# Windowed attention on one core: query norm factors moved from the queries to the scores, and ALiBi distances formed by GpSimd two steps ahead

## The chip, the cores and the metric

One core of a Trainium2 chip runs the whole program. The metric is the device time of one execution in microseconds (us), as the median of several executions of the same compiled program. Five engines work beside each other: TensorE (PE, matmuls; PEld are its weight loads), VectorE (DVE), ScalarE (ACT), GpSimd (POOL) and SyncE (SP, which here issues transfers). Each takes its own instructions strictly in the order in which they were written for it, and waits on semaphores for what the others produce.

## The reference

Two layers on a 1024 x 1024 activation in float32. Layer 0 mixes tokens with a short gated convolution, layer 1 with sliding-window attention; each is followed by a SwiGLU block. What the change touches is the attention of layer 1:

```python
q = rmsnorm(q, q_gain)      # per head of 64
k = rmsnorm(k, k_gain)
scores = jnp.einsum('bnqkgd,bnskd->bnkgqs', qb, kw) * scale
dist = qi + BLOCK - kj      # 0 <= dist < 128 is kept
scores = scores - slopes * dist          # per query head
logits = concat([where(mask, scores, -inf), sink])
p = softmax(logits)[..., :-1]
out = einsum(p, v) @ w_o
```

Sixteen query heads of 64 share four key and value heads. The RMS norm of a query is one factor per head and token. It multiplies every score of that query, so that it can be applied before the product with the keys or after it.

## The kernel before

**Arithmetic.** Each float32 product is made of matmuls on two rounded pieces per operand, a high one and the remainder: a "split" is a cast to the high piece and a subtraction that gives the low one. Large projections use a scheme of seven products for eight.

**The stage.** The attention lies between about 985 and 1262 us of the span. First the keys, the values and the first query tiles are projected (`first_pairs`, until about 1027 us). Then come 64 units (i, b): i is a query tile of two heads (0 to 7), b a block of 128 queries (0 to 7). They run one per step, and since each unit's work is spread over four steps, several are under way at once. PE's time between the pieces of a unit is filled with granules of the query projection of later tiles, which is why the steps until about 1185 us carry matmuls of `three` (L1997) and the later ones carry the output projection.

**What sets the order.** The string `ORDER` (L60) is one step. Each letter calls a function on a unit, and what it issues goes into the queues of the engines in that order. For step n: S is `scores` of unit n (PE, L2234 and L2235, into one PSUM bank, P0), T is `turn` of unit n-2 (four PE transposes, L2277), M is `maxima` of unit n (DVE, L2249: score plus distance, times minus the slope, and the minimum with the sink, in one custom operation), E is `exponents` of unit n-1 (ACT, L2269), D is `divide_steps` of finished groups, H and L are `turn_hi` (ACT) and `turn_lo` (DVE, L2290) of unit n-2, V and O are `values` and `keep_o` of unit n-3, P is a piece of the projection, and k and K issue what `plan` has put on an agenda for the step or half a step before it. Since P0 is one bank, the scores of unit n+1 wait until the maxima of unit n have read it.

**The queries.** `keep_q` makes tile i ready for the scores, on the agenda after its projection is complete: squares (ACT), sums over each head (`head_stats`, L1678, PE with 2 columns), mean (`head_mean`, L1685), logarithm and exponential for a first guess (ACT), one Newton step (`head_guess` L1704 and L1706, `head_newton` L1710 and L1711, DVE with 16 columns). The factor is one number per token and head, with the tokens in the partitions, while the queries have their tokens in the columns. So the factor is spread over 512 columns by a GpSimd copy (`spread`, L1803), transposed four times by PE (`turn_blocks`, L1808) and multiplied onto the raw queries by DVE (`scale_rows`, L1813), each twice per tile. Only then are the queries split, in four parts: `part_hi` (ACT, L2165) and `part_lo` (GpSimd, L2170). The division by the sums of exponents uses the same `spread` and `turn_blocks`.

**GpSimd's other work.** It subtracts for the splits of the projection's weights (`split_granule`, L1941; the cast ahead of it, L1940, is on DVE or ACT), for the keys (L1878) and for the output projection, and makes two short steps of the softmax sums (L2332 and L2334).

**Buffers of the scores.** `score_buffers` (L1815) gives three buffers of 128 x 512; unit n uses buffer n mod 3, each of its two rows of 256 columns holding 192 live ones. The distances are one constant table of 192 columns that `maxima` reads for every unit.

## Time and profile before

| | |
|---|---|
| median of 3 runs | 1926.03 us (1925.07 to 1926.16) |
| span of the profiled execution | 1921.5 us |
| 960 to 1027 us: PE / DVE / POOL busy | 66.92 / 40.77 / 12.94 us of 67.00 |
| 1027 to 1230 us, the 64 units: PE / DVE / POOL busy | 197.41 / 168.67 / 114.72 us of 203.00 |
| 1230 to 1262 us: PE / DVE / POOL busy | 32.00 / 25.39 / 5.80 us of 32.00 |

The span counts from the first instruction to the last and is 4.5 us below the median. Busy time is the time in which at least one instruction of an engine ran. A high share says that an engine has little room, and not yet that it sets the end; that is read from the chain of waits and from what PE waits for. In a row of a group, the numbers behind the bar are the busy time in us, the mean duration of one in ns, and the idle time of that engine just before, with what ended it.

### The profile page before, as it was taken

The page shows a single profiled execution, that of the slowest core. Times are in us where ns is not written, and L with a number is a line of the kernel's source. Part 1 is how long each engine was busy: PE and PEld are TensorE (multiplying, and loading weights), DVE is VectorE, ACT ScalarE, POOL GpSimd, SP SyncE. Part 2 cuts the span into 40 slices and gives each one's busy share as a digit, 9 for nine tenths or more (in the row PEclk, how much of TensorE's full clock was granted, in tenths as well). Part 3 has the DMA queues.
Part 4 walks back from the last instruction along what each step waited for, and adds up shares of the span by engine and source line. Part 5 has one row for each costly group of instructions (what it writes and reads, how often), then busy time and mean ns, then how long its engine had stood idle before and what let it go on. Part 6 is the DMA issues. An engine that isn't in the chain of part 4 may idle for free.

```text
span 1921.5 us, 25423 instructions
## 1 busy us (share of the span) xinstructions
PE 1910.4 (99%) x9045; PEld 1595.6 (83%) x9045; DVE 1323.1 (69%) x2293; ACT 891.6 (46%) x1753; POOL 305.9 (16%) x391
## 2 busy tenths in 40 slices
PE   9999999999999999999999999999999999999999
PEld 7888888888888888888887888888888888888887
DVE  8998877975655666555767888788756665665543
ACT  5543464633333334444557787556333333344441
POOL 0011231011111100000015556310111111100000
PEclk9999999999999999999999999999999999999999
DMA  8896695387888647986374661232675575477562
GB/s 317 258 251 149 133 249 160 110 274 209 228 250 234 152 141 281 325 249 211 102 257 158 210 214 50 94 137 89 216 204 144 196 200 158 130 251 269 198 228 100
DMA packets 154910, 374.13 MB, mean 195 GB/s; under 512 B 15392, under 2 KB 26784, under 8 KB 154784
## 3 DMA queue, kind: packets, MB, share of 16 engines
q1 hardware_dynamic: 119392, 263.16, 40.1%
q0 software_dynamic: 35248, 109.33, 23.4%
q8 instruction: 71, 1.16, 0.2%
q14 instruction: 55, 0.45, 0.1%
q10 hardware_dynamic: 144, 0.03, 0.0%
HBM read 300.89 MB, written 149.42 MB: 234 GB/s over the span
## 4 chain that ended last, share of the span: by engine, by line
PE 96%; DVE 2%; ACT 1%; issue 1%; POOL 0%; DMA 0%; SPq 0%; POOLq 0%; ACTq 0%; DVEq 0%
PE acc L1004 16%; PE acc L1007 16%; PE acc L1005 16%; PE P L1004 10%; PE P L1005 10%; PE P L1007 10%; PE acc L172 3%; PE acc L1997 2%; PE P L1997 2%; PE acc L176 1%; PE P L2277 1%; PE P L1678 1%; PE P L1808 1%; PE acc L1137 1%; PE acc L1139 1%; PE acc L1138 1%
## 5 line engine op out<-in xcount | busy, mean ns | idle before, releaser
L1004 PE MATMUL acc<-XS,G 128*128 128x512 f32 x926 | 360.4, 389 | 0.0
L1005 PE MATMUL acc<-XS,G 128*128 128x512 f32 x926 | 360.2, 389 | 0.0
L1007 PE MATMUL acc<-XS,G 128*128 128x512 f32 x926 | 360.2, 389 | 0.0
L1004 PE MATMUL P<-A,G 128*128 128x512 f32 x550 | 214.1, 389 | 0.0
L1007 PE MATMUL P<-A,G 128*128 128x512 f32 x550 | 214.0, 389 | 0.0
L1005 PE MATMUL P<-A,G 128*128 128x512 f32 x550 | 214.0, 389 | 0.0
L1007 PEld LDWEIGHTS acc<-XS,G 128*128 128x128 f32 x926 | 173.8, 188 | 36.2
L1005 PEld LDWEIGHTS acc<-XS,G 128*128 128x128 f32 x926 | 173.8, 188 | 36.1
L1004 PEld LDWEIGHTS acc<-XS,G 128*128 128x128 f32 x926 | 173.8, 188 | 36.0
L1004 PE MATMUL acc<-A,G 128*128 128x512 f32 x442 | 172.1, 389 | 0.0
L1007 PE MATMUL acc<-A,G 128*128 128x512 f32 x442 | 172.0, 389 | 0.0
L1005 PE MATMUL acc<-A,G 128*128 128x512 f32 x442 | 171.9, 389 | 0.0
L938 DVE TENSOR_TENSOR G<-WL,G 128x512 fp32r<-128x512 f32 x168 | 115.2, 685 | 73.2 <-ACT G L937 73.2
L938 DVE TENSOR_TENSOR G<-WR,G 128x512 fp32r<-128x512 f32 (+1 forms) x216 | 144.4, 668 | 30.6 <-ACT G L937 30.6
L937 ACT CAST G<-WR 128x512 fp32r<-128x512 f32 (+1 forms) x216 | 130.5, 605 | 62.3 <-PE acc L1007 31.4
L937 ACT CAST G<-WH 128x512 fp32r<-128x512 f32 (+1 forms) x174 | 104.6, 601 | 88.5 <-PE acc L1007 38.2
L938 DVE TENSOR_TENSOR G<-WH,G 128x512 fp32r<-128x512 f32 (+1 forms) x174 | 115.6, 665 | 23.3 <-ACT G L937 23.2
L1339 ACT ACTIVATE G<-G 128x512 f32<-128x512 f32 x88 | 55.8, 634 | 158.5 <-DVE G L1436 152.7
L1007 PEld LDWEIGHTS P<-A,G 128*128 128x128 f32 x550 | 103.2, 188 | 21.5
L1004 PEld LDWEIGHTS P<-A,G 128*128 128x128 f32 x550 | 103.2, 188 | 21.4
L1005 PEld LDWEIGHTS P<-A,G 128*128 128x128 f32 x550 | 103.2, 188 | 21.4
L901 POOL DMA_DIRECT2D s<-s x68 | 60.0, 892 | 365.3 <-DMA s<-s 179.5
(414 smaller groups left out, 3794.2 us busy)
## 6 DMA issues: line engine op xcount, KB each, us to landing
G<-h SPq DMA_DIRECT2D x70, 512.0 KB, 4.5
s<-in_w_dn SPq DMA_DIRECT2D x32, 704.0 KB, 8.4
h<-X POOLq DMA_DIRECT2D x44, 512.0 KB, 4.8
s<-s POOLq DMA_DIRECT2D x32, 704.0 KB, 7.1
WR<-s SPq DMA_DIRECT2D x79, 256.0 KB, 3.9
WR<-in_w_gu SPq DMA_DIRECT2D x36, 512.0 KB, 5.1
WH<-in_w_gu SPq DMA_DIRECT2D x36, 512.0 KB, 4.2
XS<-q_ops SPq DMA_DIRECT2D x36, 512.0 KB, 5.1
```

Of the source, the lines that this page charges most:

```text
L172: pe.matmul(ps.half(h), wh, xs[:, j, c], start=first and j == 0, stop=False)
L176: pe.matmul(ps.half(h), wl, xs[:, 0, c], start=False, stop=last)
L901: nc.gpsimd.dma_start(dst[to], dst[of], accum_op=ALU.add)
L937: lambda: act.copy(out_hi, raw),
L938: lambda: lo_eng.tensor_tensor(out_lo, raw, plain(out_hi), ALU.subtract),
L1004: pe.matmul(ps, w[:, 0, c], x[:, 0, :], start=start and e == 0, stop=False, skip_group_check=True)
L1005: pe.matmul(ps, w[:, 0, c], x[:, 1, :], start=False, stop=False, skip_group_check=True)
L1007: pe.matmul(ps, w[:, 1, c], x[:, 0, :], start=False, stop=last, skip_group_check=True)
L1137: pe.matmul(ps, hi[:, kc], xs[:, 0, c], start=k == 0, stop=False, skip_group_check=True)
L1138: pe.matmul(ps, hi[:, kc], xs[:, 1, c], start=False, stop=False, skip_group_check=True)
L1339: state["silu"] = act.activation(x, x, AF.Silu)
L1997: pe.matmul(ps, g[:, w, c], x[:, b, :], start=begin and i == 0, stop=end and i == 2, skip_group_check=True)
```

## The change

The query factor is not multiplied onto the queries any more. The raw queries are split and multiplied with the keys, and the factor is applied where the scores leave PSUM. With r the factor, x the raw score, s the slope and d the distance, the softmax needs s*d - r*x up to its sign. The constant table of distances holds -d. The new `maxima` computes (x - d*a) * (-r), with a = s/r, so that the custom operation keeps its form: its second operand is now -d*a, a table of its own for every unit, and its multiplier is -r, one number per query.

- `query_mean` (four DVE operations of 64 x 8 columns) takes the place of `head_mean` for queries, since the mean must now lie with sub-block and head arranged as the scores' partitions are. For it, `eps_q` is laid out once by four small DVE copies. `query_newton` gives -r and, by one more operation, `away` = a. The multiplication by the inverse slope (L1706) is gone.
- The spreads, transposes and multiplications of the query factor are gone: per tile two L1803, two groups of four L1808, two L1813.
- `distances` is new: for every unit one GpSimd operation (two narrower ones for b = 0) writes -d*a into the unit's score buffer. The letter A ahead of `ORDER` issues it for unit n+2 in step n.
- The buffers become five: s0, the two halves of G2 and the two halves of X7, the last tile of the residual. X7 is therefore stored aside to memory about 9 us after the stage's start and loaded back in the output projection; from then on the two late buffers lie in XS0. Maxima and exponents run in place.
- The query parts are issued some three steps earlier after their projection.

```diff
-ORDER = "SPTMEDkPHLVOPK"
+ORDER = "ASPTMEDkPHLVOPK"
...
-        def head_guess(y, inv):
+        def head_guess(y):
...
-            if inv is not None:
-                dve.tensor_tensor(y, y, inv.unsqueeze(1).to_broadcast([P, NB, 2]), ALU.mult)
...
+        def query_mean(st):
+
+            m = slot("hr_m", (P, NB, 2), bufs=2)
+            src = st[:, 0 : 2 * NB].rearrange("p (b h) -> p b h", h=2)
+            for e in range(2):
+                to = slice(e * SUB, (e + 1) * SUB)
+                for sub in range(2):
+                    of = slice(sub * SUB, (sub + 1) * SUB)
+                    dve.scalar_tensor_tensor(m[to, :, sub], src[of, :, e], 1.0 / HD, it["eps_q"][to, :, sub], ALU.mult, ALU.add)
+            return m
+
+        def query_newton(i, y, t, m):
+
+            dve.scalar_tensor_tensor(t, t, 0.5, m, ALU.mult, ALU.mult)
+            dve.scalar_tensor_tensor(y, t, 1.5, y, ALU.subtract, ALU.mult)
+            minus[i] = y
+            away[i] = slot("away", (P, NB, 2), bufs=3)
+            dve.scalar_tensor_tensor(away[i], m, cst[:, C_NEGS + i : C_NEGS + i + 1], y, ALU.mult, ALU.mult)
...
-        def scale_rows(raw, wide, q, pb):
-            turn_blocks(pb, wide)
-            c = slice(q * 512, q * 512 + 512)
-            dve.tensor_tensor(raw[:, c], raw[:, c], pb, ALU.mult)
...
         def score_buffers():
-            g2 = slot("G2")
-            s_bufs.append(slot("s0", (P, 2, 2 * P)))
-            s_bufs.extend(g2[:, h * 512 : h * 512 + 512].rearrange("p (e c) -> p e c", e=2) for h in (0, 1))
+            s_bufs.append(slot("s0", (P, HALF)))
+            for tag in ("G2", f"X{NK - 1}"):
+                both = slot(tag)
+                s_bufs.extend((both[:, lo_half], both[:, hi_half]))
...
+            at(t + 9.0, lambda: nc.sync.dma_start(x_aside, X[NK - 1]))
...
-            for d, f in ((0, first.rows1), (1, first.hi2), (1.5, first.hi3), (2, first.lo2), (3, first.lo3)):
+            for d, f in ((0.5, first.hi2), (1, first.hi3), (1.5, first.lo2), (3, first.lo3)):
...
-                (rows[0] - 1.5, [lambda: wide_of(0)]),
-                (rows[0] - 0.5, [lambda: wide_of(1)]),
-                (rows[0], [lambda: rows_of(0)]),
-                (rows[0] + 0.5, [lambda: part_hi(0, 0)]),
-                (rows[1], [lambda: rows_of(1), lambda: part_lo(0, 0)]),
...
+            for n, (h, e) in enumerate(((0, 0), (0, 1), (1, 0), (1, 1))):
+                d = later + hold + 2 + n + 0.5 * (n > 0)
+                plan(d, lambda h=h, e=e: part_hi(h, e))
+                plan(d + (0.5 if n else 1), lambda h=h, e=e: part_lo(h, e))
...
+        def distances(i, b):
+            if b == 0:
+                for sub in (0, 1):
+                    _, n = sub_keys(b, sub)
+                    far = away[i][:, b, sub : sub + 1].to_broadcast([P, n])
+                    pool.tensor_tensor(live_parts(i, b)[:, sub, KEYS - n :], dist[:, KEYS - n :], far, ALU.mult)
+                return
+            far = away[i][:, b, :].unsqueeze(2).to_broadcast([P, 2, KEYS])
+            pool.tensor_tensor(live_parts(i, b), dist.unsqueeze(1).to_broadcast([P, 2, KEYS]), far, ALU.mult)
...
                     u["ps"][:, sub, 0:n],
-                    dist[:, KEYS - n :],
-                    cst[:, C_NEGS + i : C_NEGS + i + 1],
+                    live,
+                    minus[i][:, b, sub : sub + 1],
...
+                "A": lambda: at(-2, distances),
```

How the instructions move is seen in the queues. In a row stand the line, the operation, the tiles written and read with their shape, and how often it repeats. Line numbers of the changed kernel are higher: L1808 stays in the divisions as L1827, L1941 is now L1980, L2170 is L2207, L2277 is L2305, L1997 is L2036.

On **PE**, a step in the sixteen units of tiles 2 and 3 before: the transposes of a score tile (from cst, the identity, and G, a score buffer), behind them those of the spread query factor, then projection matmuls (`acc`) and the values.

```order
L1997 MATMUL acc_8414<-XS_1101_7500,WL_7847 128x512 x2
L2277 MATMUL P_1261_8892<-cst_61,G_1187_8365 128x128 x4
L1808 MATMUL P_1262_8904<-cst_61,G_1244_8764 128x128 x4
L1997 MATMUL acc_8414<-XS_1101_7500,WL_7847 128x512
L1997 MATMUL acc_8414<-XS_1106_7534,WL_7847 128x512
L2303 MATMUL acc_8416<-G_1258_8871,A_1181_8306 128x256
```

The same projection matmuls in the changed kernel:

```order
L2036 MATMUL acc_8417<-XS_1101_7501,WL_7848 128x512 x2
L2305 MATMUL P_1263_8903<-cst_61,s_1188_8374 128x128 x4
L2036 MATMUL acc_8417<-XS_1101_7501,WL_7848 128x512
L2036 MATMUL acc_8417<-XS_1106_7535,WL_7848 128x512
L2331 MATMUL acc_8419<-G_1260_8881,A_1182_8313 128x256
```

The second group of four is gone and the rest keeps its place. In the whole program PE's queue goes from 8337 to 8320 rows with 64 transposes fewer; 13 of the 16 groups stood directly behind a `turn` like this one, and three stood alone.

On **POOL**, the stretch from one weight split (L1941) to the spread of a division (L1803 from `den`) before, with the spread of a query factor (L1803 from `hr_y`) and the two short steps on `mx` and `den`:

```order
L1941 TENSOR_TENSOR WL_7846<-WR_7842,WL_7846 128x512
L1803 COPY G_1279_9036<-hr_y_9111 128x512
L2332 TENSOR_TENSOR mx_8596<-mx_8596,cst_61 128x16
L2334 TENSOR_TENSOR den_8630<-den_8630,mx_8596 128x16
L1803 COPY G_1279_9036<-hr_y_9111 128x512
L1941 TENSOR_TENSOR WL_7847<-WR_7842,WL_7847 128x512
L1803 COPY s_1310_9232<-den_8630 128x512
```

The same stretch in the changed kernel, with the distances (L2264, from cst, the table, and `away`) and two query parts (L2207):

```order
L1980 TENSOR_TENSOR WL_7847<-WR_7843,WL_7847 128x512
L2264 TENSOR_TENSOR X_1190_8376<-cst_61,away_8858 128x2x192
L2207 TENSOR_TENSOR G_1285_9078<-WH_7846,G_1285_9078 64x8x64
L2264 TENSOR_TENSOR s_1188_8374<-cst_61,away_8858 128x2x192
L2360 TENSOR_TENSOR mx_8604<-mx_8604,cst_61 128x16
L2362 TENSOR_TENSOR den_8638<-den_8638,mx_8604 128x16
L2207 TENSOR_TENSOR G_1285_9078<-WH_7846,G_1285_9078 64x8x64
L1980 TENSOR_TENSOR WL_7848<-WR_7843,WL_7848 128x512
L2264 TENSOR_TENSOR G_1189_8375<-cst_61,away_8858 128x2x192
L2207 TENSOR_TENSOR G_1302_9202<-WH_7846,G_1302_9202 64x8x64
L2264 TENSOR_TENSOR G_1189_8375<-cst_61,away_8858 128x2x192
L1822 COPY s_1310_9237<-den_8638 128x512
```

The two spreads are gone, four distances stand between what was there, and the query parts come ahead of the division's spread where they came behind it. Over the program POOL gets 56 operations of L2264 and 16 narrower ones (L2261).

On **DVE**, the Newton step of one query tile before, between a `turn_lo` (L2290), a `keep_o` (L2322) and the next maxima (L2249, shown as ISA):

```order
L1685 SCALAR_TENSOR_TENSOR hr_m_8828<-P_1251_8819,eps_r_8000 128x16
L2290 TENSOR_TENSOR G_1254_8834<-P_1250_8812,G_1254_8834 128x256
L2322 TENSOR_TENSOR G_1219_8570<-acc_8416,G_1219_8570 64x2x2x64
L1704 TENSOR_TENSOR hr_t_8847<-hr_y_8830 128x16
L1706 TENSOR_TENSOR hr_y_8830<-hr_y_8830,cst_61 128x16
L1710 SCALAR_TENSOR_TENSOR hr_t_8847<-hr_t_8847,hr_m_8828 128x16
L1711 SCALAR_TENSOR_TENSOR hr_y_8830<-hr_t_8847,hr_y_8830 128x16
L2249 ISA G_1187_8365,mx_8471<-P_1256_8853,cst_61 128x192
```

And in the changed kernel, at the same place:

```order
L1719 SCALAR_TENSOR_TENSOR hr_m_8832<-P_1252_8823,eps_q_8005 64x8 x4
L2318 TENSOR_TENSOR G_1255_8841<-P_1251_8816,G_1255_8841 128x256
L2350 TENSOR_TENSOR G_1220_8577<-acc_8419,G_1220_8577 64x2x2x64
L1704 TENSOR_TENSOR hr_t_8854<-hr_y_8837 128x16
L1724 SCALAR_TENSOR_TENSOR hr_t_8854<-hr_t_8854,hr_m_8832 128x16
L1725 SCALAR_TENSOR_TENSOR hr_y_8837<-hr_t_8854,hr_y_8837 128x16
L1728 SCALAR_TENSOR_TENSOR away_8858<-hr_m_8832,cst_61,hr_y_8837 128x16
L2276 ISA G_1189_8375,mx_8472<-P_1258_8862,G_1189_8375,cst_61,hr_y_8567 128x192
```

The mean is four operations for one, the slope's multiplication has gone, `away` has come, and the maxima stand behind the same four small operations.

More of the change, by code (lines that the diff above doesn't have):

```diff
@@ L41 @@
 C_KG = C_QG + 1
-C_INVS = C_KG + 1
-C_NEGS = C_INVS + NH
+C_NEGS = C_KG + 1
 C_ONES = C_NEGS + NK
@@ L1863, in token_rows @@
                 dve.tensor_scalar(it["eps"], m, EPS, None, ALU.mult)
+                it["eps_q"] = slot("eps_q", (P, NB, 2))
+                for e in range(2):
+                    for sub in range(2):
+                        of = it["eps"][sub * SUB : (sub + 1) * SUB, :]
+                        dve.tensor_copy(it["eps_q"][e * SUB : (e + 1) * SUB, :, sub], of)
                 rsqrt(it["r"], m, (P, NB))
@@ L2075, in first_pairs @@
                     if (j, p) == (12, 2):
-                        for d, f in ((0.1, first.mean), (0.5, first.guess), (0.9, first.newton), (1.2, first.wide0), (2.9, first.wide1)):
+                        for d, f in ((0.1, first.mean), (0.5, first.guess), (0.9, first.newton)):
                             at(line.end + d, f)
-                    if p == 1 and j == 13:
-                        line.work(2, first.rows0)
                 t = line.end
@@ L2116, in first_pairs, with keep_q @@
             t = line.end
[L2117 to L2120 removed]
+            at(t - 1.6, first.hi0)
+            at(t - 0.9, first.lo0)
+            at(t - 0.8, first.hi1)
+            at(t - 0.1, first.lo1)
             for pair in (0, 1):
                 at(t + 0.1, keep_v, 1, pair)
[L2123 removed]
+            for d, f in ((0.5, first.hi2), (1, first.hi3), (1.5, first.lo2), (3, first.lo3)):
                 agenda.setdefault(d, []).append(f)
[L2126 removed]
+        def keep_q(i, raw_of, side=None, later=0, hold=0, steps=False):
             t = {}
@@ L2170, in part_lo @@
                 eng.tensor_tensor(q[rest, :, e, :], raw_half(h, rows), plain(q)[rows, :, e, :], ALU.subtract)
-            rows_of = lambda h: scale_rows(t["raw"], t["side"][h], h, bank(pos["free"]))
-            wide_of = lambda h: spread(pool, t["side"][h], t["y"][:, 4 * h : 4 * h + 4, :])
             if steps:
-                shared = lambda h: spread(act, t["side"][h], t["y"][:, 4 * h : 4 * h + 4, :])
                 return SimpleNamespace(
@@ L2371, in attention_layer @@
         NU = len(units)
-        pos = {"n": -LAG, "step": 0, "free": "P1", "piece": 0, "values": None}
+        pos = {"late": NU, "n": -LAG, "step": 0, "free": "P1", "piece": 0, "values": None}
         agenda = {}
@@ L2513, in attention_layer @@
             run(work)
+            pos["late"] = pos["n"] + 2
+            another_buffer()
             pos["values"] = None
```

72 lines of the change are left out of this document (35 added, 37 removed).

## The prediction

> **What bounds the kernel now.** I read the first section of the page, then the chain of work that ended last.
>
> ```profile
> span 1921.5 us, 25423 instructions
> PE 1910.4 (99%) x9045; PEld 1595.6 (83%) x9045; DVE 1323.1 (69%) x2293; ACT 891.6 (46%) x1753; POOL 305.9 (16%) x391
> PE 96%; DVE 2%; ACT 1%; issue 1%; POOL 0%; DMA 0%; SPq 0%; POOLq 0%; ACTq 0%; DVEq 0%
> ```
>
> TensorE is busy for 99% of the span and is 96% of the chain, so PE work that goes is worth its time, and work elsewhere counts only where PE comes to wait for it. The span is 4.5 us below the median of 1926.03 us. I sum against the span and add 4.5 us at the end.
>
> The averages hide the stage that is changed, so the next view is the busy time by stretches: in each row the length, then PE, PEld, DVE, ACT and POOL busy, the granted clock and the DMA share.
>
> ```profile
> 1027.00:1052.00 25.00, 22.05 (x140) 18.36 (x139) 20.26 (x59) 20.04 (x52) 17.65 (x13) 1.00 0.45 166
> ...
> 1061.00:1109.00 48.00, 47.60 (x334) 42.80 (x334) 42.33 (x130) 37.62 (x118) 25.15 (x28) 1.00 0.63 206
> ...
> 1143.00:1170.00 27.00, 26.42 (x180) 23.23 (x180) 23.77 (x66) 23.53 (x72) 21.32 (x21) 1.00 0.27 89
> ```
>
> Here DVE is at 88% (42.33 of 48.00) and not at 69%, and POOL at 52%, in two stretches at 71 and 79%, and not at 16%. PE has little slack in any of them. The third view is what PE waits for between 960 and 1270 us: total us, times, longest.
>
> ```profile
> PE P L2234 <- DVE mx L2249: 2.4, 4, 1.0
> PE acc L1997 <- POOL WL L1941: 1.7, 2, 1.4
> PE P L2234 <- POOL G L2170: 0.5, 1, 0.5
> PE P L1808 <- DVE A L2350: 0.3, 1, 0.3
> PE P L1678 <- DVE G L2290: 0.3, 1, 0.3
> PE acc L1997 <- issue: 0.3, 1, 0.3
> ```
>
> They sum to 5.5 us. There is no large wait to win; the certain gain is PE work that disappears.
>
> **Term 1, the transposes.** What a group of four costs is read from starts and not from modelled ends. PE's order in time, with start and duration:
>
> ```profile
> 1098.30 0.26 PE L2234 MATMUL P<-A,G 128*128 128x192 f32 x1
> ...
> 1099.21 0.60 PE L2277 MATMUL P<-cst,s 128*128 128x128 f32 x4
> 1099.56 0.48 PE L1997 MATMUL acc<-XS,WL 128*128 128x512 f32 x1
> ...
> 1100.83 0.19 PE L2234 MATMUL P<-A,G 128*128 128x64 f32 x1
> ...
> 1101.74 0.60 PE L2277 MATMUL P<-cst,G 128*128 128x128 f32 x4
> 1102.18 0.60 PE L1808 MATMUL P<-cst,s 128*128 128x128 f32 x4
> 1102.54 0.70 PE L1997 MATMUL acc<-XS,WL 128*128 128x512 f32 x2
> ...
> 1103.78 0.25 PE L2234 MATMUL P<-A,G 128*128 128x192 f32 x1
> ```
>
> A lone group takes 1099.56 - 1099.21 = 0.35 us, one with a second group behind it 1102.54 - 1101.74 = 0.80 us, so the second costs 0.45. Of the sixteen groups that go, 13 stand behind a `turn` and 3 alone: 13 x 0.45 + 3 x 0.35 = **6.9 us**. PE is the bound, and nothing hides this.
>
> **Term 2, waits that go with the old query path.** Splitting the queries no longer waits for spread, transposes and product, and comes some three steps earlier; a step is 2.53 to 2.95 us by the three starts of L2234 above. The wait for `part_lo` (0.5) should go. DVE loses the products with the spread factor from the queue in which the maxima stand:
>
> ```profile
> L1813 DVE TENSOR_TENSOR G<-G,P 128x512 f32<-128x512 f32 x8 | 5.5, 685 | 2.7 <-PE P L1808 2.5
> L1706 DVE TENSOR_TENSOR hr_y<-hr_y,cst 128x16 f32<-128x16 f32 x8 | 1.4, 175 | 0.3
> L1704 DVE TENSOR_TENSOR hr_t<-hr_y 128x16 f32<-128x16 f32 x10 | 1.9, 185 | 1.7 <-ACT hr_y L1702 1.6
> L1940 DVE CAST WL<-WR 128x512 fp32r<-128x512 f32 x20 | 11.0, 548 | 1.6 <-DMA WR<-in_w_q 1.3
> ```
>
> Sixteen products at 0.685 and eight L1706 at 0.175 are 12.4 us of DVE. Those that stood between two maxima made some of the 2.4 us of waiting for `mx`; with the bounds at 0 and 2.4 I take 1.0, since four waits face sixteen products. Together **1.5 us**. The waits for weight splits (1.7) stay: they are POOL's, and POOL gets more to do.
>
> **Term 3, POOL.** No operation like `distances` is in the trace. The nearest rows:
>
> ```profile
> L1941 POOL TENSOR_TENSOR WL<-WR,WL 128x512 fp32r<-128x512 f32 x22 | 28.6, 1302 | 40.1 <-ACT WL L1940 11.0 <-DVE WL L1940 8.7 <-PE P L2277 8.1
> L147 POOL TENSOR_TENSOR WL<-WR,WH 128x256 fp32r<-128x256 f32 x14 | 10.2, 737 | 18.7 <-ACT WH L144 18.5
> L1803 POOL COPY G<-hr_y 128x512 f32<-128x512 f32 x12 | 7.2, 611 | 12.0 <-PE P L1808 6.1 <-DVE hr_y L1711 5.8
> ```
>
> Two-operand work costs 1.302 us for 512 columns and 0.737 for 256, so (1.302 - 0.737) / 256 = 2.2 ns a column, and 384 columns 0.737 + 128 x 0.0022 = 1.02 us. The operation reads one operand broadcast along a row, as the L1803 copy does; if that made it a one-operand operation it would be no more than 0.61, and if it cost as much as 512 columns 1.30. I take 1.02, from the two rows of its own kind.
>
> In 1061 to 1109 us lie 48.00 / 2.74 = 17.5 steps, by the mean of the two steps above. POOL then has 25.15 - 4 x 0.61 + 17.5 x 1.02 = 40.6 us, 85% (69% and 95% at the bounds). It fits. In 1027 to 1052 us, nine units, it has 17.65 - 2 x 0.61 + 9 x 1.02 = 25.6 of 25: full, at the beginning, where no lead has been built up. In 1143 to 1170 us it has 21.32 - 2 x 0.61 + 9.5 x 1.02 = 29.8 of 27, over by 2.8, against a lead of two steps, about 5.5 us. The lead covers the second place by itself; in both POOL's queue is in order, so a weight split or a `part_lo` behind a distance is late when the distance is. I put **1.0 us** of new PE waits on POOL, near the 0.6 at the start.
>
> **Term 4, DVE against POOL.** The trace shows that some operations of the two exclude each other. From the timelines of DVE and POOL:
>
> ```profile
> 1028.34 0.43 DVE L1940 CAST WL<-WR 128x512 fp32r<-128x512 f32 x1
> ...
> 1029.00 1.29 POOL L1941 TENSOR_TENSOR WL<-WR,WL 128x512 fp32r<-128x512 f32 x1 [1.56 <-DVE WL L1940]
> 1029.28 1.29 DVE L1940 CAST WL<-WR 128x512 fp32r<-128x512 f32 x1
> ...
> 1159.02 1.31 POOL L2432 TENSOR_TENSOR XS<-G,XS 128x512 fp32r<-128x512 f32 x1
> ...
> 1160.06 0.30 DVE L1704 TENSOR_TENSOR hr_t<-hr_y 128x16 f32<-128x16 f32 x1
> ```
>
> The same cast takes 0.43 us free and 1.29 beside a POOL subtraction that ends at 1030.29, 0.28 us before the cast. A Newton operation takes 0.30 where its group's mean is 0.185, beside a POOL operation that ends at 1160.33. So a blocked operation waits out the other's. Casts average 0.548 - 0.43 = 0.12 us of this with POOL about half busy; at 85% I estimate 0.4, thus 20 x 0.28 = 6 us more on DVE. The Newton chain of a tile has four operations that read two tiles from SBUF (L1704 and, new in form or number, L1724, L1725, L1728). If two meet a distance of 1.02 us halfway, the chain is 1.0 us late, 8 us in all. The four-part mean and `away` add 8 x 4 x 0.175 = 5.6 us. DVE's balance is -12.4 + 6 + 8 + 5.6 = +7 us on 203 us: not a bound by its sum. What counts is where the chain stands, just ahead of maxima for which PE's next scores wait.
>
> ```profile
> 1099.70 0.47 DVE L2249 CUSTOM_DVE_ANT_0 G<-P,cst 128x192 f32<-128x192 f32 x1
> ```
>
> This last maximum of a unit ends at 1100.17, and the next scores start at 1100.83: a cover of 0.66 us. A chain late by 1.0 exceeds it by about 0.4, for eight tiles **3.2 us** (0 if every operation slips between two of POOL's; upward in the rival below).
>
> The Trainium skill bears on this, "SBUF — State Buffer", section "Who interferes with whom": VectorE's second pair of SBUF ports is GpSimd's, and the one that starts first locks it for the whole instruction, against VectorE operations with two SBUF inputs and those in two-port modes. The two pairs of times above agree. By that rule maxima, with one input in PSUM, are not blocked, and each of the chain's four operations can be blocked anew, which is the rival on the slower side.
>
> **Edits at nothing.** The store of X7 aside, some 9 us into the stage, and its load in the output projection are two transfers more on SP's queue, and loads of projection operands stand behind the first.
>
> ```profile
> 990.00:1000.00 10.00, 10.00 (x58) 8.57 (x57) 4.46 (x10) 5.37 (x12) 0.00 (x0) 1.00 0.89 330
> 1000.00:1010.00 10.00, 10.00 (x58) 8.56 (x58) 4.85 (x8) 4.92 (x10) 2.57 (x2) 1.00 0.16 39
> 1185.00:1230.00 45.00, 44.95 (x291) 39.35 (x290) 35.86 (x102) 33.83 (x107) 18.97 (x24) 1.00 0.11 36
> ```
>
> The first comes into the fullest stretch (share 0.89, 330 GB/s), where its 0.5 MB take about 1.6 us, and behind it the share falls to 0.16 while PE is full in both rows; the second meets a share of 0.11. Both are hidden; a wait for one would cost about 1.6 us. The custom operation keeps its form and length. Distances that wait for a buffer stand two steps behind the last transpose from it, so the five buffers cost nothing unless POOL runs ahead.
>
> **Sum.** -6.9 - 1.5 + 1.0 + 3.2 = -4.2 us: 1921.5 - 4.2 + 4.5 = **1921.8 us**.
>
> **Rivals.**
> *POOL becomes the bound.* For it: it is full in 1027 to 1052 and over in 1143 to 1170 us, and it idled 40.1 us ahead of its weight splits because its queue is in order, idle time that distances cannot all fill. Against: 85% in between, and the lead. With 1.30 us a distance, the first place is 17.65 - 1.2 + 9 x 1.30 = 28.2 of 25, 3.2 us late with no lead, and the second 32.5 of 27, as much as the lead; with 3.2 at the first and some 2 at the second in place of 1.0, the total is near 1926. Between the two prices lies 1924 to 1927.
>
> *The lock makes DVE late, and the change slower.* If POOL runs without gaps when the chain comes, an operation that was blocked lets the next distance or split start, and all four wait. The price: two whole waits and two halves of 1.02 are 3.1 us at worst; with gaps in POOL's queue 2.2 us. Beyond the cover that is 1.55 x 8 = 12.4 in place of 3.2, so -8.4 + 1.0 + 12.4 = +5 us, about 1931. It decides from a chain that is late by 0.66 + 8.4 / 8 = 1.7 us. Against it: POOL at 85% is not without gaps, and ACT steps between the mean and the guess give it time to run dry.
>
> *All gain is kept.* POOL's lead covers both places, the chain slips through, and the old waits go but for 0.3 of issue: -6.9 - 5.2 = -12.1, 1913.9 us. Against: the two waits for weight splits are POOL's own.
>
> **How the numbers follow.** Forecast 0.42 with 1918 to 1924.5; POOL bound 0.25; lock 0.20; full gain 0.13. The range 1914.5 to 1930.5 cuts the ends of the last two. A difference of 0.2%, 3.9 us, is about what a measurement can tell, so faster means below 1922.2: the full gain and some 0.31 of the forecast, 0.44. Within 0.2%: the rest of the forecast and most of POOL, 0.33. Slower, above 1929.9: the lock and POOL's tail, 0.23.
>
> **What would show it.** L1808's count down by 64 and PE's busy time by about 7 us (term 1). No wait of scores for `part_lo` (term 2). L2264 at 1.02 us, POOL near 85% in the middle of the stage, and no PE wait for a distance through the maxima (term 3). Casts near 0.8 us, Newton operations at 0.3 to 1.0 instead of 0.17, and PE's waits for maxima just behind them (term 4). I am wrong if a distance takes far more than 1.30 us, or if PE's waits for maxima exceed 10 us.

## The result and the profile after

The changed kernel takes 1939.38 us (median of 4 runs, 1937.54 to 1942.49) against 1925.55 us for the kernel before beside it (4 runs): a ratio of 1.0073, with an interval of 1.0059 to 1.0087. It is slower by 14 us, where 4 us faster was forecast, and outside the range. All times below are medians of fast executions; one slow execution, of e12, is left out. The first section of the page of the changed kernel, then PE's waits between 960 and 1290 us:

```profile
span 1938.4 us, 25422 instructions
PE 1915.6 (99%) x8981; PEld 1598.1 (82%) x8981; DVE 1331.7 (69%) x2305; ACT 893.1 (46%) x1751; POOL 348.2 (18%) x450
```

```profile
PE P L2249 <- DVE mx L2276: 12.2, 10, 3.2
PE acc L2036 <- POOL WL L1980: 2.5, 2, 2.3
PE P L2249 <- POOL G L2207: 1.3, 1, 1.3
PE P L1678 <- DVE G L2318: 0.3, 1, 0.3
PE acc L2036 <- issue: 0.2, 1, 0.2
```

The page shows little of the loss: PE is still at 99%, and POOL's busy time is up by 42 us, the distances. The waits do show it: 16.5 us instead of 5.5, and 9.8 of the 11.0 us more are for maxima. The busy time by stretches shows the other half of the loss, in the column behind the engines, the granted clock, which was 1.00 in every stretch of the profiled execution before:

```profile
1027.00:1052.00 25.00, 20.08 (x86) 16.09 (x85) 17.55 (x44) 14.17 (x37) 18.68 (x14) 0.75 0.40 143
1052.00:1061.00 9.00, 7.66 (x47) 6.57 (x47) 6.40 (x17) 7.11 (x21) 5.27 (x6) 0.93 0.17 41
1061.00:1109.00 48.00, 44.35 (x290) 38.81 (x289) 39.12 (x118) 35.92 (x109) 35.44 (x39) 0.96 0.62 207
1109.00:1157.00 48.00, 45.05 (x307) 39.55 (x306) 42.14 (x125) 38.20 (x118) 33.70 (x42) 1.00 0.65 214
1143.00:1170.00 27.00, 26.58 (x180) 23.09 (x180) 23.31 (x69) 23.07 (x70) 22.39 (x25) 1.00 0.55 179
1157.00:1185.00 28.00, 24.78 (x151) 21.76 (x150) 21.90 (x63) 20.58 (x61) 24.88 (x28) 0.88 0.27 85
```

A stretch at 0.75 loses a quarter of its time if PE is the bound: 25 x 0.25 + 9 x 0.07 + 48 x 0.04 + 28 x 0.12 = 12.2 us. So the change adds up as -6.9 us of transposes, +11.0 of waits and +12.2 of clock = +16.3, against 16.9 in the spans. PE counts as busy while it runs at half speed, which is why its share says nothing here. Its busy time does: it rises by 5.2 us (1910.4 to 1915.6) although 6.9 us of work is gone.

The new operation itself is cheaper than forecast, and the chain on DVE is the opposite (groups of POOL and DVE between 985 and 1275 us):

```profile
L2264 POOL TENSOR_TENSOR G<-cst,away 128x384 f32<-128x384 f32 x23 | 19.2, 836 | 0.9 <-PE P L2305 0.3
...
L1704 DVE TENSOR_TENSOR hr_t<-hr_y 128x16 f32<-128x16 f32 x10 | 6.0, 604 | 2.3 <-ACT hr_y L1702 2.2
L1728 DVE SCALAR_TENSOR_TENSOR away<-hr_m,cst,hr_y 128x16 f32<-128x16 f32 x8 | 6.0, 751 | 0.3
L1725 DVE SCALAR_TENSOR_TENSOR hr_y<-hr_t,hr_y 128x16 f32<-128x16 f32 x8 | 3.9, 486 | 0.3
L1724 DVE SCALAR_TENSOR_TENSOR hr_t<-hr_t,hr_m 128x16 f32<-128x16 f32 x8 | 2.5, 311 | 0.2
```

The four means add up to 2.15 us. One tile shows how, in DVE's order, then POOL's, then PE's:

```profile
1122.41 0.95 DVE L1704 TENSOR_TENSOR hr_t<-hr_y 128x16 f32<-128x16 f32 x1
1123.39 0.17 DVE L1724 SCALAR_TENSOR_TENSOR hr_t<-hr_t,hr_m 128x16 f32<-128x16 f32 x1
1123.60 0.69 DVE L1725 SCALAR_TENSOR_TENSOR hr_y<-hr_t,hr_y 128x16 f32<-128x16 f32 x1
1124.33 1.30 DVE L1728 SCALAR_TENSOR_TENSOR away<-hr_m,cst,hr_y 128x16 f32<-128x16 f32 x1
1125.66 0.48 DVE L2276 CUSTOM_DVE_ANT_0 G<-P,G,cst 128x192 f32<-128x192 f32 x1
...
1122.04 1.29 POOL L2207 TENSOR_TENSOR G<-G,G 64x512 fp32r<-64x512 f32 x1
1123.40 0.85 POOL L2264 TENSOR_TENSOR X<-cst,away 128x384 f32<-128x384 f32 x1
1124.34 1.26 POOL L2207 TENSOR_TENSOR G<-G,G 64x512 fp32r<-64x512 f32 x1
...
1126.60 0.36 PE L2249 MATMUL P<-A,G 128*128 128x192 f32 x1 [2.59 <-DVE mx L2276]
```

L1704 ends at 1123.36, just behind POOL's first operation (1123.33), L1725 at 1124.29 behind the second (1124.25), L1728 at 1125.63 behind the third (1125.60). POOL pauses for less than 0.1 us between its operations, three of the chain's four operations each wait out one of POOL's, the maxima wait behind them on DVE, and PE's next scores wait 2.59 us for the maxima.

The other tiles agree. PE's four long waits for maxima (1.85, 2.95, 2.59 and 3.16 us, 10.6 of the 12.2) each come behind a tile whose chain was 2.2 to 2.6 us late. In the two tiles where none of the four operations was held up (at 1096 and 1146 us), the waits for maxima just behind are 0.22 us at most.

### The profile page after: what moved, and what is told of

Its sections match the earlier page's. It is cut to its first block, busy times and chain, and to the rows that moved or that the text cites. A ratio compares the mean times of both kernels' runs of the same rounds, so it can differ in the third digit from the quotient of the medians.

```text
span 1938.4 us, 25422 instructions
## 1 busy us (share of the span) xinstructions
PE 1915.6 (99%) x8981; PEld 1598.1 (82%) x8981; DVE 1331.7 (69%) x2305; ACT 893.1 (46%) x1751; POOL 348.2 (18%) x450
## 4 chain that ended last, share of the span: by engine, by line
PE 94%; DVE 2%; ACT 1%; issue 1%; POOL 1%; DMA 1%; SPq 0%; POOLq 0%; ACTq 0%; DVEq 0%
PE acc L1004 16%; PE acc L1005 16%; PE acc L1007 16%; PE P L1004 10%; PE P L1007 10%; PE P L1005 10%; PE acc L171 3%; PE P L2036 2%; PE acc L2036 2%; PE acc L175 1%; PE P L2305 1%; PE acc L1137 1%; PE acc L1139 1%; PE acc L1138 1%; PE P L1678 1%
```

## The experiments

The times, against the runs of the kernel before of the same job:

| run | us | ratio (interval) |
|---|---|---|
| e1 chain on POOL | 1954.02 | 1.0151 (1.0135 to 1.0166) |
| e2 no distances | 1926.74 | 1.0006 (0.9997 to 1.0016) |
| e3 before, with POOL's load | 1936.45 | 1.0057 (1.0042 to 1.0072) |
| e4 chain in PSUM | 1934.75 | 1.0049 (1.0034 to 1.0064) |
| e5 key casts on ACT | 1935.74 | 1.0057 (1.0040 to 1.0074) |
| e7 PSUM and no distances | 1926.30 | 1.0003 (0.9993 to 1.0012) |
| e8 PSUM and key casts | 1933.49 | 1.0043 (1.0029 to 1.0057) |
| e9 head sums in two groups | 1938.29 | 1.0069 (1.0054 to 1.0084) |
| e10 chain at four places | 1933.44 | 1.0047 (1.0032 to 1.0061) |
| e11 both | 1936.17 | 1.0060 (1.0043 to 1.0077) |
| e12 both and key casts | 1935.22 | 1.0055 (1.0038 to 1.0072) |
| e13 first distances on ACT | 1935.95 | 1.0052 (1.0037 to 1.0067) |
| e14 that, and chain at four places | 1928.99 | 1.0019 (1.0009 to 1.0028) |
| e15 before, 0.9 us later | 1926.36 | 0.9999 (0.9990 to 1.0008) |
| e16 before, 1.7 us later | 1926.82 | 1.0004 (0.9995 to 1.0013) |
| e17 as e14, square on ACT | 1927.86 | 1.0014 (1.0005 to 1.0022) |
| e18 as e17, more distances on ACT | 1932.62 | 1.0043 (1.0029 to 1.0056) |
| e19 a wait of POOL for the chain | 1948.75 | 1.0127 (1.0105 to 1.0149) |

### What the load on POOL does, with and without the new chain

**e2**, the changed kernel without distances (it leaves out their division by the factor, so its result is another):

```diff
-ORDER = "ASPTMEDkPHLVOPK"
+ORDER = "SPTMEDkPHLVOPK"
...
-                    live,
+                    dist[:, KEYS - n :],
```

> The changed kernel without the operation on GpSimd: the maxima read the constant table of distances again, while the multiplier stays the query's factor (so the distances are not divided by it, and the result is another). LOCK and LOAD both: the chain meets POOL about as seldom as before the change, the transposes stay away, and the time is 1914 to 1922. A rival that lays the loss on the rest of the change (the mean in four parts, the earlier query parts, the moved residual): it stays above 1930.

12.6 us of the loss go with the distances, so they are the cause; but 1926.74 is no gain over before, though the transposes are gone. Waits of 10.6 us were left, two of them long (3.8 and 2.8 us), both behind the chain, and half clock took 3.4 us. At the first of them, DVE, then POOL:

```profile
1040.76 2.20 DVE L1704 TENSOR_TENSOR hr_t<-hr_y 128x16 f32<-128x16 f32 x1
...
1040.25 2.68 POOL L1917 TENSOR_TENSOR A<-G,A 64x1024 fp32r<-64x1024 f32 x1 [0.68 <-ACT A L1912]
```

The chain met key, query and weight subtractions even without distances. Why the kernel before hardly suffered this is seen in POOL's order there: the first spread stood right behind the chain in issue and waited for it, so POOL stood still while the chain ran.

```profile
1111.92 1.17 POOL L1803 COPY G<-hr_y 128x512 f32<-128x512 f32 x2 [1.91 <-DVE hr_y L1711]
```

The change removed the spread as work, and the wait with it. That reading is tried in e19.

**e3**, the kernel before with one POOL operation per unit, in the score buffer of the next unit:

```diff
-ORDER = "SPTMEDkPHLVOPK"
+ORDER = "SPTAMEDkPHLVOPK"
...
+        def load(i, b):
+            to = s_bufs[(i * NB + b) % 3][:, :, 0:KEYS]
+            far = cst[:, C_INVS : C_INVS + 2].unsqueeze(2).to_broadcast([P, 2, KEYS])
+            pool.tensor_tensor(to, dist.unsqueeze(1).to_broadcast([P, 2, KEYS]), far, ALU.mult)
```

> The kernel before, with one POOL operation of 128x2x192 per unit added whose result the maxima overwrite (and the layout of the score buffers of the changed kernel, so that it has room); query factors, transposes and the chain with L1706 as before. LOCK: the chains on DVE are blocked as in the changed kernel, PE waits for maxima 8 to 16 us, and the time is 1933 to 1945. If the new kernel's own parts are needed for the loss: within 4 us of before.

The time fell into the expected range, and the reason given for it was wrong: with the spreads still in place L1704 takes 0.280 us on the mean and the other three 0.17. The maxima wait for POOL directly. In the longest case POOL's operation for the unit, issued only one step ahead, stands behind a split that waits for its cast:

```profile
1031.73 0.34 DVE L2252 CUSTOM_DVE_ANT_0 s<-P,cst 128x64 f32<-128x64 f32 x1 [2.32 <-POOL s L2240]
```

So the load costs some 10 us in the old kernel too, by another path: PE's waits are 12.8 us, and 3.4 us go to half clock.

### The chain

**e1**, the chain's four operations on POOL (six there):

```diff
-            dve.scalar_tensor_tensor(t, t, 0.5, m, ALU.mult, ALU.mult)
-            dve.scalar_tensor_tensor(y, t, 1.5, y, ALU.subtract, ALU.mult)
+            pool.tensor_tensor(t, t, m, ALU.mult)
+            pool.tensor_scalar(t, t, 0.5, 1.5, ALU.mult, ALU.subtract)
+            pool.tensor_tensor(y, t, y, ALU.mult)
...
```

> The changed kernel with the Newton chain of a query tile on GpSimd: L1704, L1724, L1725 and L1728 become six small POOL operations (the form with three operands is written as two), so that nothing of the chain can be blocked by POOL. Theory LOCK (each DVE operation of the chain that reads two SBUF tiles waits out one POOL operation, the maxima behind it are late, PE waits and its clock falls): PE's waits for maxima fall from 12.2 us to under 4, the granted clock in 1157 to 1185 us rises from 0.88 to near 1, and the time falls by 8 to 14 us, to 1925 to 1931. Rival LOAD (POOL simply has too much to do, distances and splits come late): POOL gets some 8 x 1.2 us more, and the time stays at 1939 or rises by up to 5.

PE's waits for maxima fell to 5.8 us, the way LOCK says though not under 4, and the kernel became 15 us slower than the change. POOL, whose queue is in order, now waits for ACT's exponential, and behind it stand the short steps of the softmax sums, for which ACT waits in turn. ACT's waits for them in e1, 4.6 us in the changed kernel:

```profile
ACT mx L2363 <- POOL mx L2362: 22.1, 6, 4.8
```

**e19**, a wait of POOL in the place of the removed spread:

```diff
                 query_newton(i, t["y"], t["t"], t["m"])
+                if i:
+                    pool.tensor_copy(away[i], away[i])
```

> The changed kernel with one small POOL operation per tile (1 to 7), a copy of the factor a onto itself, right behind the chain in the order of issue, where the kernel before had the first spread. POOL's queue is in order, so POOL stands still there until the chain is done. Theory FENCE (the removed spread waited for the chain, 1.6 to 1.9 us in the steady part, and so kept POOL quiet while the chain ran; without it POOL's operations run on and block the chain one by one): the four operations' mean times together fall from 2.15 us to under 1.3, PE's waits for maxima from 12.2 to 5 to 8 us, and the time by 4 to 10 us, to 1929 to 1935. If POOL's load alone makes the chain late: POOL stands still 10 us more, the waits stay or grow, and the time is 1939 or more.

The mechanism holds and the cure doesn't: the time was expected to fall by 4 to 10 us and rose by 9. The four means fall from 2.15 to 0.239 + 0.312 + 0.176 + 0.348 = 1.08 us and PE's waits for maxima to 8.1. But ACT waits 20.5 us for the short steps on POOL, as in e1. Before the change POOL could afford to stand still for the chain (ACT's waits of this kind were 3.8 us); with a distance per unit it can't.

**e4**, no chain operation with two inputs in SBUF (tiles 1 to 6):

```diff
+            ps = rooms["banks"][3][:, 2 * P : 2 * P + 4 * NB].rearrange("p (n b h) -> p n b h", n=2, h=2)
+            return ps[:, 0], ps[:, 1]
...
+                act.activation(t, y, AF.Square)
...
-            dve.scalar_tensor_tensor(t, t, 0.5, m, ALU.mult, ALU.mult)
+            dve.scalar_tensor_tensor(room, t, 0.5, m, ALU.mult, ALU.mult)
```

> The changed kernel with the chain of tiles 1 to 6 written so that none of its DVE operations reads two SBUF tiles: the mean and the half-way product lie in PSUM (in the free half of the bank of the values), the square is one more ACT operation of 128x16. POOL's work and its order stay as they are. LOCK: the chain's operations take 0.17 to 0.25 us each, PE's waits for maxima fall from 12.2 to under 5 us, less clock is lost, and the time is 1922 to 1930. If POOL's load hurts in another way (late distances, late splits): the chain gets short, yet PE waits elsewhere, and the time stays above 1933.

> The same chain in PSUM, and no distances on POOL (the maxima read the constant table, so the distances are not divided by the factor). In the run without distances alone, two waits of 3.8 and 2.8 us were left, both behind a chain blocked by key parts and splits. LOCK: these go, and with 6.9 us of transposes less than before the time is 1915 to 1920. If the gain of the transposes isn't real: it stays near 1926.

> The chain in PSUM together with the late key casts on ACT. If the two losses are separate, the gains add: e4's time less 2 to 4 us, 1919 to 1927. If the early wait for the key split only moves: e4's time within 2 us.

The chain is free, with POOL's load as it was: the same operation, by where its input lies.

```profile
L1737 DVE SCALAR_TENSOR_TENSOR away<-acc,cst,hr_y 128x16 f32<-128x16 f32 x6 | 1.4, 234 | 0.2
L1737 DVE SCALAR_TENSOR_TENSOR away<-hr_m,cst,hr_y 128x16 f32<-128x16 f32 x2 | 1.8, 918 | 0.1
```

0.234 us from PSUM (`acc`) and 0.918 for the two tiles left in SBUF. The same six tiles took 0.70 on the mean in the changed kernel and 1.30 at most. So LOCK is shown. PE's waits for maxima went from 12.2 to 1.5 us, which leaves late distances no more than 1.5 of them. The time fell by 4.6 us only, and not to 1922 to 1930, since the shared bank brought waits of its own (2.8 us of values for ACT's logarithm, which reads it) and half clock lost as much as in the changed kernel, about 12 us. e7, the same without distances, has 6.3 us of waits in all, hardly more than the 5.5 before, 6.9 us less work by the forecast's count, and takes as long as before, where 1915 to 1920 was expected. Half clock took 6.8 us, as much as the gain, in stretches like this one, where the profiled execution before had 1.00.

```profile
1061.00:1109.00 48.00, 47.47 (x304) 41.53 (x304) 38.92 (x120) 37.85 (x117) 21.63 (x23) 0.94 0.61 195
```

In e8, with the key casts on ACT too, the time is 1.3 us below e4, no more than the spread of the runs, where 2 to 4 us were expected if the gains add.

**e10**, the four operations half a step apart:

```diff
-            for d, f in ((1, lambda: squares(0)), (1.5, lambda: squares(1)), (2.5, stats_of), (2.5, mean), (3, guess), (3, newton)):
+            for d, f in ((1, lambda: squares(0)), (1.5, lambda: squares(1)), (2.5, stats_of), (2.5, mean), (3, guess), (3.5, lambda: newton(0)), (4, lambda: newton(1)), (4.5, lambda: newton(2))):
```

> The changed kernel with the chain's four DVE operations at four places, half a step apart, each alone between others; POOL's work, the head sums and everything else as they are. LOCK: each operation can still be blocked by one POOL operation, but one block of at most 1.3 us at a time is mostly covered; PE's waits for maxima fall from 12.2 to under 5 us, and the time by 6 to 12 us, to 1927 to 1933. If the place behind the maxima of a chain doesn't matter: 1937 to 1941.

PE's waits for maxima fall to 4.9 us and the time by 6 us, while the operations stay blocked (the first takes 0.600 us on the mean, the last 0.625). A block of one POOL operation is mostly covered; three in a row are not.

### The start of the units, and the clock

**e5**, three key casts on ACT, and **e13**, the distances of the first ten units on ACT:

```diff
-                    dve.tensor_copy(hi[rest, e, :], raw[rows, :])
+                    (dve.tensor_copy if (g, e) == (0, 0) else act.copy)(hi[rest, e, :], raw[rows, :])
```

```diff
+            if i * NB + b < 10:
+                for sub in (0, 1):
+                    _, n = sub_keys(b, sub)
+                    act.activation(live_parts(i, b)[:, sub, KEYS - n :], dist[:, KEYS - n :], AF.Copy, scale=away[i][:, b, sub : sub + 1])
+                return
```

> The changed kernel with the three late key casts (L1914) on ACT instead of DVE. One of them takes 2.05 us beside a POOL subtraction, ahead of PE's longest single wait for a weight split (2.3 us), after which the clock is half for 10 us. Theory KEYS (that wait costs some 2 us and some 5 us of clock): the time falls by 4 to 8 us, to 1931 to 1935. If the clock falls anyway, as the next long wait brings it down: a fall of at most 2 us.

> The changed kernel with the distances of the first ten units on ACT (two copies with a factor per partition for each unit) instead of POOL; the rest as it is. Theory START (POOL is full from 1027 to 1060 us, so the key split and a query part are late there, 2.5 and 1.3 us of waits in the changed kernel, and half clock follows for some 10 us): these waits fall to before's 1.7 and 0.5 us or less, little half clock is left before 1060 us, and the time falls by 6 to 10 us, to 1929 to 1933. If the early waits are the key casts' own: within 3 us of 1939.

e5 gave 3.6 us, a little under the 4 to 8 expected, with the wait for the weight split behind the key casts still at 1.9. In the profiled execution it gained clock (0.80 in place of 0.75 at the start, 0.94 in place of 0.88 at 1157 to 1185 us, 3.6 us in all) and 2.4 us of waits (those for maxima went from 12.2 to 9.5). e13 brought the early waits to 1.8 and 0.5 us, about those of before, and the clock to 0.86; the time fell by 3.4 us, not 6 to 10, because later stretches lost more clock than in the changed kernel (0.93 and 0.96).

**e9**, **e11** and **e12**, the head sums in two groups:

```diff
-            for d, f in ((1, lambda: squares(0)), (1.5, lambda: squares(1)), (2.5, stats_of), (2.5, mean), (3, guess), (3, newton)):
+            for d, f in ((1, lambda: squares(0)), (1.5, lambda: squares(1)), (2.5, lambda: stats_of(0, 4)), (3, lambda: stats_of(4, 4)), (3, mean), (3.5, guess), (3.5, newton)):
```

> The changed kernel with the sixteen head sums of a tile (L1678, two columns each, 0.11 us apart) in two groups of eight half a step apart, and the chain half a step later; the four operations of the chain stay together. Theory CLOCK (a wait for maxima does the clock harm because it comes just behind the head sums, so that PE's array does little for some 3.4 us): the waits for maxima stay at 8 or more us, but less time passes at half clock from 1061 us on (in the changed kernel about 10 us, of which half is lost), and the time falls by 4 to 8 us, to 1931 to 1935. If long waits alone bring the clock down: the half clock stays as long, and the time within 3 us of 1939.

> Head sums in two groups and the chain at four places. If LOCK and CLOCK are the two halves of the loss: little half clock after 1061 us, waits for maxima under 5 us, and 1922 to 1928. If POOL's load has a price beyond both: above 1931.

> The last one and the late key casts on ACT. If the early wait for the key split still costs clock: 2 to 4 us below the last one, 1919 to 1926, which is at or below the kernel before. If the early wait only moves, as it did with the chain in PSUM: within 2 us of the last one.

The diff is that of e9; e11 has the four places of e10 in it, e12 the casts of e5 too. CLOCK in this form is not borne out: in e9 half clock after 1061 us lost 4.6 us by the stretches, against 5.3 in the changed kernel. The waits for maxima fell to 4.4, where 8 were expected, and other waits rose to 10. With the chain spread (e11) two groups cost 3 us more than one: half clock after 1061 us is as in e10 (3.6 us), and the waits for maxima are 7.9 us, not under 5. In e12 half clock falls to 5 us in all, and waits of 14 us keep it at 1935.

**e15** and **e16** delay the kernel before and do nothing else:

```diff
-                turn_blocks(s["rows"], s["side", g][:, halves_of[q]])
+                for _ in range(3 if (g, q) == (1, 0) else 1):
+                    turn_blocks(s["rows"], s["side", g][:, halves_of[q]])
```

> The kernel before with one group of four key transposes done three times (eight transposes more, 0.9 us by 0.11 us each), some 20 us ahead of the units; nothing else. Theory PHASE (the clock is judged in fixed stretches of some 3.4 us; the same sequence of work costs half clock or not by where it falls, and the kernel before lies well): the delay alone brings half clock in pieces of 3.4 us, each worth 1.7 us, in this run or the next, so one of them is 1.5 us or more above its delay. Against it: both are slower by their delay alone, 0.9 and 1.7 us, with a clock of 1.00 throughout.

> As the last one, with the group done five times: sixteen transposes more, 1.7 us. PHASE: half clock in one of the two at least, with 1.7 us for each piece of 3.4 us. Against it: 1.7 us slower, full clock.

By the times PHASE misses: both medians are within the spread of before (25 runs from 1923.5 to 1928.5 us). The profiled executions differ in the clock all the same. The same short wait and sixteen head sums, in the kernel before and in e15, with the matmuls behind them:

```profile
1059.30 1.95 PE L1678 MATMUL P<-cst,G 128*128 128x2 f32 x16 [0.31 <-DVE G L2290]
1061.11 0.71 PE L1997 MATMUL acc<-XS,WL 128*128 128x512 f32 x2
...
1062.14 0.62 PE L1997 MATMUL acc<-XS,WL 128*128 128x512 f32 x2
```

```profile
1060.47 1.95 PE L1678 MATMUL P<-cst,G 128*128 128x2 f32 x16 [0.31 <-DVE G L2291]
1062.27 0.70 PE L1997 MATMUL acc<-XS,WL 128*128 128x512 f32 x2
...
1063.40 1.05 PE L1997 MATMUL acc<-XS,WL 128*128 128x512 f32 x2
```

And e15's busy time by stretches of 1 us there (the clock is the third number from the end):

```profile
1063.00:1064.00 1.00, 1.00 (x6) 0.90 (x6) 0.42 (x1) 0.68 (x4) 0.44 (x1) 0.57 0.92 367
1064.00:1065.00 1.00, 1.00 (x6) 0.90 (x5) 0.89 (x5) 1.00 (x6) 0.00 (x0) 0.50 0.79 322
1065.00:1066.00 1.00, 1.00 (x5) 0.70 (x5) 0.76 (x4) 0.00 (x0) 0.79 (x2) 0.50 0.62 98
1066.00:1067.00 1.00, 1.00 (x7) 0.95 (x6) 0.18 (x2) 0.12 (x1) 0.38 (x1) 0.73 0.88 324
```

The pair of 512-column matmuls takes 0.62 us in the one and 1.05 in the other. The profiled execution of e15 has half clock twice, for 3.4 us each time, which loses 1.7 us each, and its span is 1921.5 + 0.9 + 3.4, less 1.0 of shorter waits, which is 1924.8 against 1924.4 measured. The profiled execution of e16 has a clock of 1.00 throughout, and 1923.3 is 1921.5 plus its delay. So the same work in the same order ran at half clock in one execution and at full clock in another. That the delay made the difference is not shown, since by their mean clocks the executions of the kernel before do both without any delay. Of its 81 executions beside these runs 29 have a mean clock of 1.000 and spans of 1921.2 to 1923.0 us, and 47 have 0.997 or 0.998 and spans of 1922.9 to 1926.3 us. At 1.000 are four of ten executions of e15 and four of ten of e16. The profile of the kernel before is thus of one of its full-clock executions. The changed kernel was at 0.994 or 0.995 in all four.

### Repairs together

> The same, and the chain at four places as in the run that had it alone (1933.4). If START and LOCK are separate losses, the gains add: 1923 to 1928. If what remains is clock, wherever the waits lie: 1929 to 1934.

> The run with the first distances on ACT and the chain at four places (1929.0), and the chain's first operation, the square, on ACT. In that run the square was blocked for 2.25 us by a key subtraction, with 1.5 us of PE's wait behind it and half clock before it. LOCK: that wait goes, PE's waits for maxima fall from 6.3 to under 5 us, and the time is 1925 to 1929. If ACT is too full there: no gain.

> The last one, and of the later units those with b = 2 and 5 get their distances on ACT too, a quarter of POOL's remaining ones. If POOL's load still delays something (its own late splits, the short steps for which ACT waits): 1 to 3 us below the last one, perhaps below the kernel before. If ACT has no room (it is at 77 to 82% there): the same or slower.

e14 joins the diffs of e13 and e10, and their gains (3.4 and 5.9) add: 1928.99, 10 us below the changed kernel. e17 also takes L1704 to ACT (`act.activation(t, y, AF.Square)`) and comes to 1927.86, 1.1 us less. Its waits for maxima stay at 6.2 us where under 5 was expected; waits are 10.1 us in all and half clock 1.7, against 8.6 and 5.3 in e14. e18 adds `or b % 3 == 2` to e13's condition: POOL's load falls, ACT rises from 38.33 to 39.37 of 48 us in 1061 to 1109, and it is 4.8 us slower. Half clock takes 7.3 us there and waits 11.7; that the load on ACT is the cause is not shown. No version with distances beats the kernel before.

The sum of transposes, waits and half clock does not close in these runs as it does in the changed kernel. In e2 it gives -6.9 + 5.1 + 3.4 = +1.6 us where the spans differ by +3.2, in e17 -6.9 + 4.6 + 1.7 = -0.6 where they differ by +4.1. Where the rest lies stays open.

## Why the prediction was wrong

- **Term 1 (-6.9 us)** went as put in its count, 64 + 16 transposes of L1827 where 144 of L1808 were. Its size is seen only in the sums, which close to 0.6 us in the changed kernel and less well in later runs.
- **Term 2 (-1.5 us)** did not come. The wait of scores for `part_lo` rose from 0.5 to 1.3 us. It was 0.5 in e2 too, so that the earlier issue did not remove it even without the distances; and the gain on maxima drowned.
- **Term 3 (+1.0 us on POOL)** had the mechanism and a mean price near enough: 0.84 us for a distance where 1.02 was taken, and 0.6 for the start was too little. Splits and query parts wait 1.6 us longer there (2.5 + 1.3 against 1.7 + 0.5), and e13 showed that the distances make these waits. The overload at 1143 to 1170 us did not show: the clock is 1.00 there and PE waits no more. In 1061 to 1109 us POOL was at 74% (35.44 of 48), not 85.
- **Term 4 (+3.2 us)** is the step that failed in its own mechanism. "If two meet a distance of 1.02 us halfway, the chain is 1.0 us late" was 1.5 us on the mean of the eight tiles (2.26 a tile less 0.76 by the shortest of each), and 2.2 to 2.6 us in the four tiles behind which PE waited. Waits for maxima rose by 9.8 us, to 12.2, past the 10 that the prediction names as a sign of being wrong. I had weighed POOL's share (85%) and not what stood in its queue just there: the removed spread had held POOL still during the chain, and in its place came query parts and distances. The row of L1803 in the prediction has it: 5.8 us of POOL's idle time ended by `hr_y` of L1711, the chain's last operation. The casts, the other part of this term, did not get slower (L1979: 0.535 us on the mean, 0.548 before, 0.8 expected).
- **The rival of the lock** is what happened, in half of the tiles: 2.2 us late and +12.4 us in place of 3.2, with the net at +5. By the waits it would have been right (-6.9 + 11.0 = +4.1). It was 8 us short because neither it nor any other term had a price for the clock. The **step missing** is that the rows of before show 1.00 everywhere, and I took this as given for other timings. 12.2 us, more than the added waits, came from it. (The rival's turning point of 1.7 us leaves out term 3; with its +1.0 it is 0.66 + 7.4 / 8 = 1.6.)
- **The 4.5 us added at the end** were not one thing. In the 81 executions of the kernel before the time is 2.2 us above the span; the other 2.3 us fit a profile taken in a full-clock execution, while most executions of that kernel lose some clock. The clock thus differed before anything was changed.
- **The edits at nothing** (the residual stored aside, five buffers) cost nothing that the waits show.

The Trainium skill, "SBUF — State Buffer", section "Who interferes with whom", is borne out by e4: the chain's operations with one input in PSUM run free beside the same POOL load. On the clock it has a rule in "TensorE: Matmul & The Clock Gate", section "Part 1: The HAM clock gate (the "warmup" mystery)": the clock is full or half, judged on activity in a free-running window of 3413 ns. The 0.50 in stretches of about 3.4 us agrees, and a window that runs free of the program would let one kernel have executions with and without half clock, as the kernel before has; no run here tests that cause. Which amount of work in a window keeps the clock full is not settled here: a wait of 2.59 us left it at 1.00 (1124 to 1127 us), and in e15 half clock came behind one of 0.31 us with head sums.

## What to carry to other kernels

Before work is removed, look at what it waited for: a transfer or copy that made an engine stand still may have been keeping a shared resource free for a chain elsewhere, and an engine's mean share does not show that. A chain of short DVE operations with two SBUF inputs beside a POOL without gaps can pay one POOL operation for each; put an input into PSUM, or set the operations apart. Read the granted clock beside the waits, in more than one execution of the kernel: here 11.0 us of added waits came with 12.2 us of half clock, and a profile at 1.00 was not what most executions of the same kernel got.

## What the runs showed of the hardware that was not expected

Half clock came in stretches of 3.4 us or twice or three times that (1036.2 to 1046.4 us, after the wait of 2.26 us), and in e15 and e10 behind no more than 0.3 us of waiting and sixteen matmuls of two columns. The same kernel had executions with half clock and without. GpSimd's multiplication with both operands broadcast takes 0.84 us for 384 columns, less than the line through 256 and 512 columns gives (1.02), and ACT forms 192 of the same columns in 0.446 us.
